# Two more feature pairs of the up projection by seven products of half-width blocks

## The chip, the cores and the metric

One core of a Trainium2 chip runs the whole program. TensorE (PE in the rows, PEld for its weight loads) multiplies, VectorE (DVE) and ScalarE (ACT) do the elementwise work and read PSUM, GpSimd (POOL) does small arithmetic and issues some transfers, SyncE (SP) issues most of the transfers. The metric is the device time of one execution in microseconds, as the median of several.

## The reference

Two layers on 512 tokens of width 1024. The part that matters here is the second half of a layer:

```
def conv_ffn(h, w_up, conv_w, conv_b, w_down):
    u = h @ w_up                        # (512, 1024) @ (1024, 5632)
    u = depthwise_conv3(u) + conv_b     # over tokens, three taps
    a, g = jnp.split(u, 2, axis=-1)     # 22 blocks of 128 features each
    return (jax.nn.gelu(g) * a) @ w_down
...
for l in range(2):
    x = x + gated_parallel_mixer(rmsnorm(x), ...)
    x = x + conv_ffn(rmsnorm(x), ...)
return rmsnorm(x)
```

Everything is float32. Each operand of a product is split into a high part in the fast matmul format (fp32r) and a low part, the rest; a product is the sum of high by high, low by high and high by low, three matmuls for each block of 128 along the contraction.

## The kernel before

The 1024 features of `h` lie as 8 tiles of 128 partitions by 512 tokens, each as a pair (high, low). The FFN width is cut into 22 blocks of 128 features; block f of the plain half ("a") has the number f, that of the gate half ("g") the number 22 + f. `schedule` writes the whole layer as one list of steps by hand, and a parallel list of weight blocks ("specs") in the order in which TensorE uses them. TensorE and SyncE keep that written order (`manual_schedule`). In the stretch of the change VectorE and ScalarE don't: a scheduler orders their instructions when the program is built, by priorities that the code gives (`high_priority`), and that order is then fixed; each engine takes its instructions one after another.

**A normal step** (`("up", f)`, `do_up`) takes one weight block of 1024 by 128: 8 blocks of the contraction by 3 matmuls of 128x512, into one PSUM bank. Then `conv` runs on the block: ScalarE writes the middle tap and the bias into `c` (L1113), VectorE adds the two outer taps (L1115, L1116), ScalarE takes the gelu of a gate block (L1120), VectorE multiplies it with the plain block (`prod`, L215), and after every second block `operands` makes from `prod` the split operands (`ft`) for the down projection (L1141 to L1155).

**A step by seven products** (`("us", i, p)`, `do_us`) computes two neighbouring blocks, 2i and 2i+1, at once. The contraction is cut in its even and its odd blocks (four each), the output in two feature blocks, and the tokens in two halves of 256, so that the result is a 2 by 2 product of blocks, done as 7 products instead of 8. Each product is 4 blocks by 3 matmuls of 128x256. It uses four PSUM banks; the pieces are gathered by ScalarE (L1071 to L1081) and VectorE (L1075, L1079, L1084) in two tiles `u`, of which there are two, and `conv` then reads `u`. The three matmuls of a block are these:

```
mm(ps, wh, hi, ...)    # L1066: high weights, high operand
mm(ps, wh, lo, ...)    # L1067
mm(ps, wl, hi, ...)    # L1068: the low part of the weights
```

The weights of the seven products are, in order, V11, S1, V12, S2, S4, V22 and S3. The V are blocks of the matrix, the S are sums of them. `load_sum` fetches V22 and V11 into tiles `own` (4 of them), V21 into a tile `s` and a tile `raw`, V12 into a `raw` (3 of them); POOL issues two transfers that add in place (V22 onto `s`, which gives S1, L173; V11 onto the second V21, which gives S3, L174); VectorE makes S2 from S1 and V11 (L189) and S4 from S2 and V12 (L192). So in rows `own`, `s` and `raw` as the source of a `wlo` tell which product it is for: own, s, raw, s, raw, own, raw.

**The weight split.** Every spec, normal or of a product, goes through `split`: ScalarE writes the high part `whi` (L208), VectorE the low part `wlo` (L209). There are three tiles of each, so a split can run at most three specs ahead of TensorE: the part for a spec is written when the matmuls of the third spec before it are done. A normal block is 128x1024, a block of a product 128x512.

**The operands of `us`**: `whole` copies the h tiles together into `hx` (8 ScalarE copies, L1025, and 8 transfers by POOL that add the low part in place, L1026), and `mix` makes from each of the four pairs of tiles the sums that the seven products need (`hs`, from `sums4`, L1044 to L1049). They are made once in a layer, beside the blocks 13 and 14, and serve every `us` of the layer.

Order of the second part of the up projection in a layer: after four steps of the down projection (`("sum", 0, m)`) come 13a, 13g, 14a, 14g, ..., 17a, 17g, then 18a, 19a, the one `us` for 18g and 19g, then 20a, 20g, 21a, 21g, and then `cover` and `rest` of the down projection.

**Banks.** `banks` sets for each stage which of the 8 PSUM banks a group of results goes through in turn. `do_mla_open` sets it at the start of a layer: `g` for the first four results (`ps_g`), `d` for the following, `r` for the sums of the norm.

**The constant**: `self.eps` is one column of the tile `cst`; its first reader is ScalarE in `norm_direct` (L495), in the FFN.

Of the kernel before, what the change touches and what calls it, by code (L numbers as in the profile page):

```python
# [24 lines left out]
EPS = 1e-6  # L25
# [14 lines left out]
NP, AHEAD, EVAC = (6, 5, 4), (7, 4), 400  # L40
F2 = 2 * NP[0]
FIX = 6
UPS = ((9, 1),)
ORDERS = (("V11", "S1", "V12", "S2", "S4", "V22", "S3"), ("V11", "V12", "S1", "S2", "S4", "V22", "S3"))
B11, B21, B22, T1, T3, T2, T4 = range(7)
ROWS = (slice(0, 64), slice(64, 128))
# [19 lines left out]
class Trunk:  # L66
# [5 lines left out]
    def __init__(self, ctx, tc, d):  # L72
        self.tc, self.nc, self.d, self.ctx = tc, tc.nc, d, ctx
        nc = self.nc
        self.small = ctx.enter_context(tc.tile_pool(name="small", bufs=1))
        self.const = ctx.enter_context(tc.tile_pool(name="const", bufs=1))
        self.wp = ctx.enter_context(tc.tile_pool(name="wp", bufs=1))
        self.psum = ctx.enter_context(tc.tile_pool(name="psum", bufs=1, space=bass.MemoryType.PSUM))
        self.groups, self.turn = {}, {}
        c = self.const  # L80
        x0 = c.tile([P, S + NPC], F32, name="x0")
        self.x = [x0[:, :S]] + [c.tile([P, S], F32, name=f"x{k}") for k in range(1, KD)]
        self.par = [x0[:, S:], self.small.tile([P, NPC], F32, name="par1")]
        self.early = c.tile([P, P], F32, tag="acc", name="early")
        nc.vector.memset(self.early, 1.0)
        self.idf = c.tile([P, P], F32, name="idf")
        make_identity(nc, self.idf)
        self.mean = c.tile([P, P], F32R, name="mean")
        cst = self.small.tile([P, 7], F32, name="cst")
        self.neghalf, self.ones = cst[:, 0:4], cst[:, 4:5]  # L90
        nc.vector.memset(self.neghalf, -0.5)
        nc.vector.memset(self.ones, 1.0)
        self.eps = cst[:, 6:7]
        nc.vector.memset(self.eps, EPS)
        self.warm = cst[:, 5:6]
        nc.scalar.activation(self.warm, self.ones, AF.Exp)
        self.specs, self.raws, self.parts, self.used = [], {}, [], 0
        self.plans = [self.schedule(l) for l in range(L)]
        for s, W in self.plans:
            self.specs += [w for item in s for w in W.get(item, ())]  # L100
        nc.sync.dma_start(x0[:, :S + PC_CW], d["x0"])
        self.fetch(1, 0)
        for k in range(1, 5):
            nc.sync.dma_start(self.x[k], d["xT"][k * P:(k + 1) * P, :])
            self.fetch(min(k + 1, 3), 0)
        self.gmask = self.small.tile([P, 3 * P], BF16, name="gmask")
# [223 lines left out]
    def schedule(self, l):  # L330
# [30 lines left out]
        for f in ups[8:]:  # L361
            W["up", f] = [(d["w_up"][l], 0, KD, f * P, P)]
        for i, p in UPS:
            unit = {"w": d["w_up"][l], "m": p * NF + 2 * i, "part": 1, "np": 4, "r0": 0, "order": ORDERS[0]}
# [33 lines left out]
        seq[n - 8:n - 8] = [("sum", 0, m) for m in range(0, KD, 2)]  # L398
        for i, p in UPS:
            old = [("up", p * NF + 2 * i + e) for e in range(2)]  # L400
# [97 lines left out]


    def do_mla_open(self):  # L500
        self.banks(g=[0, 1, 2, 3], d=[4, 5, 0, 1, 2, 3], r=[6, 7])
        self.mxs, self.mx = self.open("mx")
        self.mps, self.mp = self.open("ml")
        self.mp2 = self.mps.enter_context(self.tc.tile_pool(name=f"mm{self.l}", bufs=1, reuse_waits="tile"))
        self.rc, self.rsn = (self.mp.tile([P, S], F32, tag=t, name="rope", bufs=2) for t in ("knh", "knl"))
        if self.l:
            self.rope_table()
        self.hb = self.small.tile([P, 24], F32, tag="hb", name="hb")
        self.nc.vector.tensor_scalar(self.hb, self.pr[:, PC_BG:PC_BG + 24], 0.5, None, ALU.mult)
        self.merged, self.z = [None] * KD, {}  # L510
        self.qn, self.kn, self.pts, self.pp, self.y = {}, {}, {}, {}, {}
# [27 lines left out]
    def do_lat4(self):  # L539
        if self.l == 0:  # L540
            rest = self.par[0][:, PC_CW:]
            for t, src in ((rest, self.d["par"][0][:, PC_CW:]), (self.par[1], self.d["par"][1])):
                self.nc.gpsimd.tensor_copy(t[:, 0:4], self.rt)
                self.nc.gpsimd.dma_start(t, src)
            self.nc.gpsimd.tensor_scalar(self.mean, self.idf, 0.0, 1.0 / D, ALU.mult, ALU.add)
        self.latent(4, self.dense(self.spec(), self.h))

# [609 lines left out]
    def do_sum(self, part, m):  # L1157
# [33 lines left out]
        elif m == KD - 2:  # L1191
# [3 lines left out]
            for _ in self.operands(F2):  # L1195
                pass
            if UPS:
                self.whole()
# [219 lines left out]
```

## Time and profile before

| | |
|---|---|
| median of 3 runs | 1665.04 us (1664.78 to 1665.18) |
| the profiled execution: its time | 1664.89 us |
| its span, first to last instruction | 1663.1 us |
| PE busy | 1654.7 us, 99% of the span, 9480 matmuls |
| DVE busy | 1291.4 us, 78%, 2256 instructions |
| ACT busy | 948.3 us, 57%, 1704 instructions |
| POOL busy | 134.1 us, 8% |
| DMA | 191.22 MB, mean 115 GB/s |

A row of the timeline gives the start, the duration, the engine, the line, the operation and "out<-in" by the program's names with the shape; in square brackets stands how long the engine was idle before it and what ended that. Rows of equal instructions that follow each other are merged (x8). A duration of VectorE or ScalarE overlaps a little with the next instruction's, so that what an instruction takes of its queue is read from the distance of the starts. A row by windows gives, for a stretch of time, the busy time of each engine with the number of its instructions, the granted TensorE clock, the busy share of the DMA engines and GB/s.

### The profile page before, as it was taken

To read this page: it belongs to the slowest core of one execution; us is meant where nothing else is said; L and a number is where in the kernel's file an instruction comes from. 1 tells how busy PE (TensorE), PEld (TensorE's weight loads), DVE (VectorE), ACT (ScalarE), POOL (GpSimd) and SP (SyncE) were. 2 spreads that over 40 slices of the span, in tenths; PEclk is the share of its full clock that TensorE was granted. 3 is DMA by queue.
4 is the path that set the end of the run, shared out by engine and by line. 5 is a ranking of instruction groups with operands and counts; after the bars stand their busy time and mean duration, and the time that the engine had idled before them with its cause. 6 is when DMAs were issued, how large, how long until landed. Compare 5 with 4: busy or idle time off the path is not lost.

```text
span 1663.1 us, 25448 instructions
## 1 busy us (share of the span) xinstructions
PE 1654.7 (99%) x9480; PEld 1415.9 (85%) x9480; DVE 1291.4 (78%) x2256; ACT 948.3 (57%) x1704; POOL 134.1 (8%) x190
## 2 busy tenths in 40 slices
PE   9999999999999999999999999999999999999998
PEld 8888888888898889888987888888889888898888
DVE  7767866787889877797967677667878897777887
ACT  7664545775565544555566545467755655436554
POOL 2122100000000000100011220000001000001000
PEclk9999999999999999999999999999999999999999
DMA  6255523222534366636432564332236343657373
GB/s 183 74 125 114 139 84 95 77 77 74 140 97 133 101 149 155 153 96 165 110 105 80 112 146 106 98 89 77 64 85 150 90 127 101 164 131 175 96 168 94
DMA packets 326923, 191.22 MB, mean 115 GB/s; under 512 B 17072, under 2 KB 313792, under 8 KB 326800
## 3 DMA queue, kind: packets, MB, share of 16 engines
q1 hardware_dynamic: 304064, 162.38, 34.8%
q0 software_dynamic: 22448, 26.89, 9.6%
q8 instruction: 74, 1.21, 0.3%
q14 instruction: 49, 0.40, 0.1%
q10 hardware_dynamic: 288, 0.33, 0.1%
HBM read 168.80 MB, written 2.10 MB: 103 GB/s over the span
## 4 chain that ended last, share of the span: by engine, by line
PE 97%; DVE 1%; ACT 1%; issue 0%; DVEq 0%; ACTq 0%
PE ps_ring L222 13%; PE ps_ring L223 12%; PE ps_ring L224 12%; PE ps_d L222 9%; PE ps_d L224 9%; PE ps_d L223 9%; PE ps_d L1177 5%; PE ps_d L1176 5%; PE ps_d L1175 5%; PE ps_g L222 2%; PE ps_g L224 2%; PE ps_g L223 2%; PE ps_ring L303 2%; PE ps_ring L290 1%; PE ps_ring L792 1%; PE ps_g L323 1%
## 5 line engine op out<-in xcount | busy, mean ns | idle before, releaser
L208 ACT CAST whi<-raw 128x1024 fp32r<-128x1024 f32 (+5 forms) x353 | 291.3, 826 | 351.2 <-PE ps_ring L223 123.4
L209 DVE TENSOR_TENSOR wlo<-raw,whi 128x1024 fp32r<-128x1024 f32 (+5 forms) x351 | 331.4, 946 | 79.4 <-ACT whi L208 77.2
L222 PE MATMUL ps_ring<-hh,whi 128*128 128x512 f32 x600 | 235.6, 393 | 0.6 <-DVE pt L761 0.3
L224 PE MATMUL ps_ring<-hh,wlo 128*128 128x512 f32 x600 | 234.0, 390 | 0.0
L223 PE MATMUL ps_ring<-hl,whi 128*128 128x512 f32 x600 | 233.7, 390 | 0.0
L222 PE MATMUL ps_d<-hh,whi 128*128 128x512 f32 x589 | 229.4, 389 | 0.0
L223 PE MATMUL ps_d<-hl,whi 128*128 128x512 f32 x589 | 229.4, 389 | 0.0
L224 PE MATMUL ps_d<-hh,wlo 128*128 128x512 f32 x589 | 229.3, 389 | 0.0
L1176 PE MATMUL ps_d<-ft,whi 128*128 128x256 f32 x546 | 154.7, 283 | 0.0
L1177 PE MATMUL ps_d<-ft,wlo 128*128 128x256 f32 x546 | 154.7, 283 | 0.0
L1175 PE MATMUL ps_d<-ft,whi 128*128 128x256 f32 x546 | 154.7, 283 | 0.0
L222 PEld LDWEIGHTS ps_ring<-hh,whi 128*128 128x128 f32 x600 | 112.7, 188 | 24.8 <-DVE pt L761 0.6
L224 PEld LDWEIGHTS ps_ring<-hh,wlo 128*128 128x128 f32 x600 | 112.7, 188 | 23.7
L223 PEld LDWEIGHTS ps_ring<-hl,whi 128*128 128x128 f32 x600 | 112.7, 188 | 23.0
L224 PEld LDWEIGHTS ps_d<-hh,wlo 128*128 128x128 f32 x589 | 110.6, 188 | 23.1
L222 PEld LDWEIGHTS ps_d<-hh,whi 128*128 128x128 f32 x589 | 110.6, 188 | 22.7
L223 PEld LDWEIGHTS ps_d<-hl,whi 128*128 128x128 f32 x589 | 110.6, 188 | 22.7
L1176 PEld LDWEIGHTS ps_d<-ft,whi 128*128 128x128 f32 x546 | 104.9, 192 | 0.2
L1175 PEld LDWEIGHTS ps_d<-ft,whi 128*128 128x128 f32 x546 | 104.9, 192 | 0.2
L1177 PEld LDWEIGHTS ps_d<-ft,wlo 128*128 128x128 f32 x546 | 104.9, 192 | 0.0
L215 DVE TENSOR_TENSOR gz<-ps_ring,rb 128x512 f32<-128x512 f32 x44 | 30.4, 691 | 63.2 <-PE ps_ring L224 63.2
L222 PE MATMUL ps_g<-hh,whi 128*128 128x512 f32 x176 | 68.9, 391 | 0.9 <-DVE x L1185 0.9
(419 smaller groups left out, 3578.8 us busy)
## 6 DMA issues: line engine op xcount, KB each, us to landing
raw<-in_w_in_dram SPq DMA_DIRECT2D x86, 512.0 KB, 4.0
raw<-in_w_up_dram SPq DMA_DIRECT2D x68, 512.0 KB, 3.8
raw<-in_w_up_dram SPq DMA_DIRECT2D x36, 256.0 KB, 2.9
raw<-in_w_down_dram SPq DMA_DIRECT2D x18, 384.0 KB, 4.9
tm<-in_namask_dram SPq DMA_DIRECT2D x16, 384.0 KB, 4.3
tm<-in_rpb_dram POOLq DMA_DIRECT2D x48, 128.0 KB, 4.7
own<-in_w_down_dram SPq DMA_DIRECT2D x16, 384.0 KB, 5.9
raw<-in_w_in_dram SPq DMA_DIRECT2D x17, 256.0 KB, 3.2
```

The lines of the kernel that those rows point to most:

```text
L208: nc.scalar.copy(hi, src)
L209: nc.vector.tensor_sub(lo, src, r32(hi))
L215: self.nc.vector.tensor_tensor(out, a, b, ALU.mult)
L222: mm(ps, sh, mh, start=first and k == 0, stop=False)
L223: mm(ps, sh, ml, start=False, stop=False)
L224: mm(ps, sl, mh, start=False, stop=last and k == n - 1)
L290: self.nc.tensor.transpose(out[2 * u + i][:, c * 64:c * 64 + 64], block[q], self.idf[q, q])
L303: self.nc.tensor.matmul(out, st[a], mv[b], start=first and t == 0, stop=last and t == 2)
L323: self.nc.tensor.matmul(self.gbank[j], w[:, j * P:(j + 1) * P], m, start=n + t == 0, stop=False)
L1175: mm(ps, wh, hi, start=fresh and i == 0, stop=False, skip_group_check=True)
L1176: mm(ps, wh, lo, start=False, stop=False, skip_group_check=True)
L1177: mm(ps, wl, hi, start=False, stop=i == n - 1, skip_group_check=True)
```

## The change

In each of the two layers the pairs 16g, 17g and 18a, 19a are computed by seven products too, beside 18g, 19g. The steps then stand as ..., 15a, 15g, 16a, 17a, `us` for 16g and 17g, `us` for 18a and 19a, `us` for 18g and 19g, 20a, 20g, 21a, 21g: three such steps in a row (below: the first, the second and the third group). The write of `eps` moves from VectorE at the very start to POOL in `do_lat4` of the first layer. In the second layer `do_mla_open` takes the banks in the order in which the last stage used them, oldest first, instead of fixed numbers.

```diff
-UPS = ((9, 1),)
+UPS = ((8, 1), (9, 0), (9, 1))
...
         self.eps = cst[:, 6:7]
-        nc.vector.memset(self.eps, EPS)
...
     def do_mla_open(self):
-        self.banks(g=[0, 1, 2, 3], d=[4, 5, 0, 1, 2, 3], r=[6, 7])
+        a = [0, 1, 2, 3, 7, 4, 5, 6]
+        if self.l:
+            a = [self.groups["d"][(self.turn["d"] + i) % 8] for i in range(8)]
+        self.banks(g=a[:4], d=[*a[5:7], *a[:4]], r=[a[7], a[4]])
...
     def do_lat4(self):
         if self.l == 0:
...
                 self.nc.gpsimd.dma_start(t, src)
+            self.nc.gpsimd.memset(self.eps, EPS)
             self.nc.gpsimd.tensor_scalar(self.mean, self.idf, 0.0, 1.0 / D, ALU.mult, ALU.add)
```

`schedule` reads `UPS`, and replaces the two normal steps of a pair by one `us` at the place of the second:

```
for i, p in UPS:
    old = [("up", p * NF + 2 * i + e) for e in range(2)]
    seq[seq.index(old[1])] = ("us", i, p)
    seq.remove(old[0])
```

What this makes of the queues is shown at three places of the first layer; the second layer reads alike. Line numbers of the changed kernel are lower by 1 from L95 to L500, higher by 2 from there to L543 and by 3 behind that (its L208 is L209 before, its L1050, L1051, L1118 and L1119 are L1047, L1048, L1115 and L1116 before).

VectorE, where the first group's weights begin. Before, from the sums of the third `mix` on (`wlo` is the low part of a normal block, 17a and then 17g):

```order
L1047 SCALAR_TENSOR_TENSOR tt<-tt,hx 128x256
L209 TENSOR_TENSOR wlo<-raw,whi 128x1024
L1048 SCALAR_TENSOR_TENSOR tt<-tt,hx 128x256
L1044 TENSOR_TENSOR tt<-hx 128x512
L1115 SCALAR_TENSOR_TENSOR c<-ps_d,x_67,c 128x511
L209 TENSOR_TENSOR hs<-tt,hs 128x512
L1116 SCALAR_TENSOR_TENSOR c<-ps_d,x_67,c 128x511
L209 TENSOR_TENSOR hs<-tt,hs 128x512
L1047 SCALAR_TENSOR_TENSOR tt<-tt,hx 128x256
L1048 SCALAR_TENSOR_TENSOR tt<-tt,hx 128x256
L209 TENSOR_TENSOR wlo<-raw,whi 128x1024
```

Now, at the same place (`own` is V11 and `s` is S1 of the first group):

```order
L1050 SCALAR_TENSOR_TENSOR tt<-tt,hx 128x256
L208 TENSOR_TENSOR wlo<-own,whi 128x512
L1051 SCALAR_TENSOR_TENSOR tt<-tt,hx 128x256
L1047 TENSOR_TENSOR tt<-hx 128x512
L1118 SCALAR_TENSOR_TENSOR c<-ps_d,x_67,c 128x511
L208 TENSOR_TENSOR hs<-tt,hs 128x512
L1119 SCALAR_TENSOR_TENSOR c<-ps_d,x_67,c 128x511
L208 TENSOR_TENSOR hs<-tt,hs 128x512
L1050 SCALAR_TENSOR_TENSOR tt<-tt,hx 128x256
L214 TENSOR_TENSOR prod<-c 128x512
L1051 SCALAR_TENSOR_TENSOR tt<-tt,hx 128x256
L208 TENSOR_TENSOR wlo<-s_7379,whi 128x512
```

Up to the first of these rows the queue of VectorE is the same in both kernels; from it on the blocks of 1024 give way to blocks of 512, and the multiplication into `prod` moves ahead of the next split.

VectorE around the last group of the layer (before, the only one), from the low part of its third product (V12) on. Before:

```order
L209 TENSOR_TENSOR wlo<-raw,whi 128x512
L1115 SCALAR_TENSOR_TENSOR c<-ps_d,x_67,c 128x511
L192 TENSOR_TENSOR raw<-s_7539,raw 128x512
L209 TENSOR_TENSOR wlo<-s_7539,whi 128x512
L1116 SCALAR_TENSOR_TENSOR c<-ps_d,x_67,c 128x511
L209 TENSOR_TENSOR wlo<-raw,whi 128x512
L1075 TENSOR_TENSOR u<-u,ps_d 128x256
```

Now, for the third group (L188 and L191 make S2 and S4, L1078 and L1087 gather results, L1158 is the end of `operands` for 16 and 17):

```order
L208 TENSOR_TENSOR wlo<-raw,whi 128x512
L1119 SCALAR_TENSOR_TENSOR c<-u,x_67,c 128x511
L1158 TENSOR_TENSOR ft<-tt,ft 128x512
L188 TENSOR_TENSOR s_7694<-s_7694,own 128x512
L1118 SCALAR_TENSOR_TENSOR c<-u,x_67,c 128x511
L1078 TENSOR_TENSOR u<-u,ps_d 128x256
L191 TENSOR_TENSOR raw<-s_7694,raw 128x512
L1119 SCALAR_TENSOR_TENSOR c<-u,x_67,c 128x511
L208 TENSOR_TENSOR wlo<-s_7694,whi 128x512
L208 TENSOR_TENSOR wlo<-raw,whi 128x512
```

Between the low part of the third product (V12) and that of the fourth (S2) there were two instructions, L1115 and L192; now there are seven, the work of the second group and of the pair 16, 17 among them.

SyncE, the transfers of the up projection after the four steps of the down projection. Before:

```order
L140 DMA raw<-in_w_up_dram 128x8x128 x12
L170 DMA own<-in_w_up_dram 128x4x128
L170 DMA s_7539<-in_w_up_dram 128x4x128
L170 DMA own<-in_w_up_dram 128x4x128
L170 DMA raw<-in_w_up_dram 128x4x128 x2
L140 DMA raw<-in_w_up_dram 128x8x128 x4
```

Now, the third group's shown up to its last `own`:

```order
L139 DMA raw<-in_w_up_dram 128x8x128 x8
L169 DMA own<-in_w_up_dram 128x4x128
L169 DMA s_7379<-in_w_up_dram 128x4x128
L169 DMA own<-in_w_up_dram 128x4x128
L169 DMA raw<-in_w_up_dram 128x4x128 x2
L169 DMA own<-in_w_up_dram 128x4x128
L169 DMA s_7527<-in_w_up_dram 128x4x128
L169 DMA own<-in_w_up_dram 128x4x128
L169 DMA raw<-in_w_up_dram 128x4x128 x2
L169 DMA own<-in_w_up_dram 128x4x128
L169 DMA s_7694<-in_w_up_dram 128x4x128
L169 DMA own<-in_w_up_dram 128x4x128
```

Four blocks of 512 KB give way to ten of 256 KB in a layer, two of them into `raw` for each group; POOL's queue gets four more transfers that add in place, behind the eight of L1026.

## The prediction

> **What bounds the kernel now.** I read the page first, for the bound and the chain that ended last; then the busy times by windows around the place of the change; then the timelines of TensorE and VectorE there.
>
> ```profile
> span 1663.1 us, 25448 instructions
> PE 1654.7 (99%) x9480; PEld 1415.9 (85%) x9480; DVE 1291.4 (78%) x2256; ACT 948.3 (57%) x1704; POOL 134.1 (8%) x190
> PE 97%; DVE 1%; ACT 1%; issue 0%; DVEq 0%; ACTq 0%
> ```
>
> TensorE is the bound nearly everywhere, 97% of the chain. So fewer matmul columns shorten the program only as long as no other queue makes TensorE wait, and a wait put into TensorE's queue is lost for good. Whether VectorE has room must be read where the change lies. The windows of the first layer are four normal steps each, then the group of seven products (745.28 to 755.35), then four normal steps (us, then busy time and number of instructions of each engine, clock, DMA share, GB/s):
>
> ```profile
> core 0: us, PE busy (x) PEld busy (x) DVE busy (x) ACT busy (x) POOL busy (x), PEclk, DMA share, GB/s
> 679.97:701.74 21.77, 21.77 (x98) 18.04 (x97) 12.88 (x19) 13.53 (x22) 7.07 (x8) 1.00 0.96 210
> 701.74:723.51 21.77, 21.77 (x97) 18.03 (x96) 21.74 (x36) 13.28 (x19) 0.49 (x1) 1.00 0.48 135
> 723.51:745.28 21.77, 21.77 (x98) 18.03 (x96) 19.09 (x30) 10.67 (x17) 1.23 (x2) 1.00 0.30 71
> 745.28:755.35 10.07, 10.07 (x85) 10.07 (x84) 7.83 (x12) 7.38 (x13) 0.00 (x0) 1.00 0.34 99
> 755.35:777.12 21.77, 21.77 (x98) 18.04 (x97) 19.00 (x27) 11.80 (x18) 0.86 (x1) 1.00 0.55 155
> ```
>
> This is the reading that decides: TensorE never stops, but VectorE works 21.74 of 21.77 us from 701.74 on. Its 78% over the span hide a stretch in which it is full. Why it is full stands in its timeline (first row: 7.80 us idle, ended by the landing of the additions into `hx`; by then it is late with all that needs them). The same row of the second layer:
>
> ```profile
> 690.75 0.69 DVE L1044 TENSOR_TENSOR tt<-hx 128x512 f32<-128x512 f32 x1 [7.80 <-DMA hx<-hl]
> ...
> 1514.48 0.69 DVE L1044 TENSOR_TENSOR tt<-hx 128x512 f32<-128x512 f32 x1 [7.59 <-DMA hx<-hl]
> ```
>
> Less 823.93 us, the distance of the two stages (1503.90 and 679.97), the second is 690.55, so both layers start this stretch alike to 0.2 us. Before the change VectorE catches up in the normal steps up to 745 and the group finds it with room. After it the first group stands where 16g would end, at 723.51: in the full stretch.
>
> **The change part by part.**
>
> *TensorE's own time.* The rows at the start of the second up stage, at the start of the group and behind it:
>
> ```profile
> 679.97 0.40 PE L222 MATMUL ps_d<-hh,whi 128*128 128x512 f32 x1
> ...
> 745.28 0.28 PE L1066 MATMUL ps_d<-hh,whi 128*128 128x256 f32 x1
> ...
> 755.35 0.40 PE L222 MATMUL ps_d<-hh,whi 128*128 128x512 f32 x1
> ```
>
> Between the first two lie 12 normal steps of 24 matmuls: 65.31 us, 5.442 us a step, 0.2268 us a matmul. The group's 84 matmuls take 10.07 us, 0.1199 each, 1.439 us a product. A pair costs 10.88 us in normal steps and 10.07 us as a group: 0.81 us saved, four pairs in two layers, **-3.25 us**. The page "TensorE: Matmul & The Clock Gate" of the Trainium skill (section Back-to-back issue gap) gives N / 2.4 + 2.5 ns for a gap, 109 and 216 ns here; by that a pair would save 48 x 0.216 - 84 x 0.109 = 1.2 us, four 4.8 us. The trace has some 11 ns more for every matmul of either width, and the sum goes by the trace.
>
> *VectorE's queue.* What an instruction takes of it is the distance of the starts:
>
> ```profile
> 715.15 0.42 DVE L1047 SCALAR_TENSOR_TENSOR tt<-tt,hx 128x256 f32<-128x256 f32 x1
> 715.49 1.22 DVE L209 TENSOR_TENSOR wlo<-raw,whi 128x1024 fp32r<-128x1024 f32 x1
> 716.62 0.43 DVE L1048 SCALAR_TENSOR_TENSOR tt<-tt,hx 128x256 f32<-128x256 f32 x1
> 716.96 0.69 DVE L1044 TENSOR_TENSOR tt<-hx 128x512 f32<-128x512 f32 x1
> 717.56 0.75 DVE L1115 SCALAR_TENSOR_TENSOR c<-ps_d,x,c 128x511 f32<-128x511 f32 x1
> 718.22 0.69 DVE L209 TENSOR_TENSOR hs<-tt,hs 128x512 fp32r<-128x512 f32 x1
> ```
>
> 0.34 us for 256 columns, 0.60 for 512, 0.66 for a tap of the convolution, 1.13 for 1024. Two normal steps give it two splits of 1024 and four taps, 2 x 1.13 + 4 x 0.66 = 4.9 us in 10.88 us. A group gives it seven splits (4.2), S2 and S4 (1.2), two gathers of 256 and one of 512 (1.28), and four taps (2.64): 9.3 us in 10.07 us, and beside that the products and operands of 16 to 19 (two `prod`, L1141, and two of 256 and four of 512 for a pair, 4.9 us). So the change trades 0.81 us of TensorE for 4.4 us of VectorE, four times, and packs it into 30 us.
>
> Now the due times. The queue up to L1047 at 715.15 is the same in both kernels, and the first new instruction, the low part of V11 of the first group, starts at 715.49 too. From there to the low part of the fourth product (S2) of the third group, 67 instructions stand in the built order: 20 low parts of 512 (17 products and three `hs`), six S sums, three `prod`, eight of `operands`, two gathers L1084, the last L1044 and the first L1141, together 41 of 512; 14 taps of seven blocks; 12 of 256. That is 41 x 0.60 + 14 x 0.66 + 12 x 0.34 = 37.9 us, and the 68th starts at 753.4 at the earliest and is done 0.69 us later. TensorE, never waiting, would be at that product after 17 products from 723.51, 747.97, and use its low part with its third matmul, at 748.2. Adding 0.1 us for the signal (below, 829.42 to 829.56) it is there at 754.2: **6.0 us late** if VectorE never idles.
>
> It idles a little, for reasons that these rows of the group before show (a gelu late, a split's high part late, a gather that waits for its product):
>
> ```profile
> 738.00 0.69 DVE L215 TENSOR_TENSOR prod<-c 128x512 f32<-128x512 f32 x1 [0.76 <-ACT c L1120]
> ...
> 751.76 0.69 DVE L209 TENSOR_TENSOR wlo<-raw,whi 128x512 fp32r<-128x512 f32 x1 [0.70 <-ACT whi L208]
> 752.74 0.42 DVE L1079 TENSOR_TENSOR u<-u,ps_d 128x256 f32<-128x256 f32 x1 [0.28 <-PE ps_d L1068]
> ```
>
> In the new order L1079 of the first group stands behind the splits of its sixth and seventh product, so VectorE waits there for the fifth product; `prod` of 17 stands right behind the taps and waits for its gelu; one split behind L1079 waits for ScalarE. With one such wait of each kind in the 67 instructions, 0.3 + 0.7 + 0.3 (half of the third, since ScalarE has most of the gather's time for it), I take 1.3 us; the ends are 0 and 3 us (all three kinds in two of the groups, 2 x 1.74 less what overlaps). So TensorE loses **7.3 us a layer, 14.6 us** (12.0 to 18). Along the way it waits in smaller pieces, first at the third product of the first group, whose low part is the 20th of the 68 and due at 726.6 where VectorE is done with it at about 726.8; the largest, about 3 us, is the last, at S2 of the third group, behind the seven instructions that now stand there. Behind it come four normal steps, in which VectorE has 5.44 us for 3.7 us of work (1.13 + 2 x 0.66 + 4.9 / 4), and nothing more is lost.
>
> *Transfers.* Ten blocks of 256 KB for four of 512 KB in a layer, in SP's written order, and four more additions on POOL:
>
> ```profile
> raw<-in_w_up_dram SPq DMA_DIRECT2D x36, 256.0 KB, 2.9
> own<-in_w_up_dram SPq DMA_DIRECT2D x4, 256.0 KB, 4.6
> s<-own POOLq DMA_DIRECT2D x2, 256.0 KB, 3.3
> ```
>
> The DMA share is 0.30 to 0.48 where they fall, so bandwidth covers them. The tightest is V12 of the second group: its `raw` is free when S3 of the first is split (about 732), it lands 3 to 4 us later and is due on VectorE at about 737. I take nothing; if it is late it moves VectorE by up to 1 us a group, which is part of the upper end. POOL's additions come behind the eight into `hx` and 3.3 us land well ahead of use: nothing.
>
> *Other banks.* At the start of the second layer TensorE's last matmul of the first, the VectorE instruction that empties its bank, and the first of the second:
>
> ```profile
> 828.41 0.28 PE L1177 MATMUL ps_d<-ft,wlo 128*128 128x256 f32 x1
> 828.73 0.69 DVE L1185 TENSOR_TENSOR x<-x,ps_d 128x512 f32<-128x512 f32 x1
> 829.56 0.47 PE L222 MATMUL ps_g<-hh,whi 128*128 128x512 f32 x1 [0.87 <-DVE x L1185]
> ```
>
> The distance is 1.15 us where 0.12 is the rule. The first four results of the layer go to banks 0 to 3, which the last step still held. Oldest first, they find empty banks: **-1.03 us**. Two more groups also move the turn by four banks, so even the fixed numbers would miss them now. The ends are 0 and -1.03.
>
> *The constant.* A row of 0.06 us leaves VectorE, which then waits for `x` anyway; on POOL it stands behind the first write of `idf`, where POOL idles 8 us:
>
> ```profile
> 0.97 0.06 DVE L94 MEMSET cst<- 128x1 f32 x1
> ...
> 3.73 0.35 DVE L468 TENSOR_SCALAR h<-x 128x256 fp32r<-128x256 f32 x1 [2.49 <-DMA x<-in_x_dram]
> ...
> 9.00 0.76 POOL masks.py:199 TENSOR_SCALAR_AFFINE_SELECT idf<-idf 128x128 f32<-128x128 f32 x1 [8.06 <-issue]
> ...
> 21.90 0.60 PE L251 MATMUL ps_r<-idf,acc 128*128 128x128 f32 x4
> ```
>
> Nothing; `idf` has 12 us of cover, without which it could cost 0.1 us.
>
> *The sum*: -3.25 - 1.03 + 14.6 = +10.3 us on the profiled execution's 1664.89, which is 0.15 below the median of the runs: 1675.2, and against the median 1675.3. Bounds: 12.0 - 4.28 gives 1672.6, 18 - 3.25 gives 1679.6.
>
> **The rivals.**
>
> *VectorE is early enough, and the columns count.* All hangs on one time, the landing of `hx`. If the eight additions landed 7.3 us earlier than 690.75, VectorE would use that idle row and be in time at the third group; the kernel would gain 4.28 us, 1660.8, about 0.26% (0.2%, some 3 us, is what a measurement of this kernel can tell from no change). For it: the transfers in that window (DMA share 0.96) would only have to be fewer. Against it: up to 695 the same transfers stand in the same order on both queues, and the groups' own come later. At some 5 us earlier the stalls that are left, 2.1 us a layer, balance the gain: 1664 to 1666.
>
> *The clock falls.* The first rows of TensorE in the trace:
>
> ```profile
> 1.05 3.36 PE L432 MATMUL idle<-early 128*128 128x128 f32 x14 [1.05 <-DVE cst L92]
> ...
> 4.44 2.04 PE L323 MATMUL ps_g<-h,whi 128*128 128x512 f32 x4
> ```
>
> After the idle start TensorE is slow: four matmuls of 512 in 2.04 us, one each 0.5 us against 0.227 later, though it has worked since 1.05, so for some 5 us. If a wait in the groups brings that state back, 5 us of products at half speed lose 2.5 us a layer, 1680.3. The longest wait that I expect, 3 us, is longer than any of the trace before, so whether it is long enough isn't shown; the granted clock of 1.00 in the windows speaks against it only for shorter ones. The same page of the Trainium skill (section HAM oscillation) has a rule for it: no idle gaps of more than about 3.4 us, or the clock halves. By that rule a wait of 3 us is just short enough.
>
> *The banks do nothing.* If the first results of the second layer wait for a weight split instead, the 1.03 us stay, 1676.3. Against it: the high part of its first block is written 3 us before (first row), only that of the third falls into the wait:
>
> ```profile
> 825.01 0.62 ACT L208 CAST whi<-raw 128x512 fp32r<-128x512 f32 x1 [1.07 <-PE ps_d L1176]
> ...
> 828.65 0.62 ACT L208 CAST whi<-raw 128x512 fp32r<-128x512 f32 x1 [1.18 <-PE ps_d L1176]
> ```
>
> **How the numbers follow.** The forecast, 0.77; VectorE early enough 0.05, or half so 0.05; the clock 0.06; the banks 0.07. Faster by over 0.2% is the first rival alone, 0.05; within 0.2% the half of it, 0.05; slower 0.90. The range takes in the bounds of the forecast, the clock and the banks, and stretches below the bound of 1672.6 for a VectorE that goes 3% faster through its queue (1.1 us a layer): 1670.4 to 1680.
>
> **What the profile after would show.** VectorE without a gap of a microsecond from 690 to about 757 in the first layer and again some 829 us later (823.93, and what the first layer loses); in the list of waits TensorE waiting for `wlo` L208 in the three groups, 7 us a layer, most of it at the fourth product of the third group; the groups at 0.12 us a matmul between the waits; no wait for L1188 (L1185 before) at the start of the second layer. I am wrong if TensorE passes the third group without waits, or if the 67 instructions take clearly other than 38 us.

## The result, and the profile after

The changed kernel takes **1678.86 us** (median of 4 runs, 1677.86 to 1679.58) where the kernel before takes 1665.10 on the same chip: a ratio of 1.0083, 95% interval 1.0065 to 1.0100. It is 13.8 us slower; the forecast was 1675.3, 10.3 us slower, and the measured time lies inside its range. The profiled execution is the one of 1679.58 us, 14.7 us above the profiled one of before.

The head of its page, the bound and the chain:

```profile
span 1677.8 us, 25906 instructions
PE 1657.4 (99%) x9624; PEld 1422.6 (85%) x9624; DVE 1307.6 (78%) x2295; ACT 962.5 (57%) x1740; POOL 141.5 (8%) x199
PE 89%; DVE 7%; issue 2%; ACT 1%; DMA 1%; POOL 0%; DVEq 0%; ACTq 0%
```

TensorE's share of the span hides the loss again, but the chain doesn't: VectorE had 1% of it before, and has 7% now. Where, the windows of the first layer say (the stretches of before; the three groups now stand from 723.46 to 762.84):

```profile
701.74:723.51 21.77, 21.77 (x98) 18.03 (x97) 21.77 (x39) 12.88 (x22) 3.45 (x4) 1.00 0.69 141
723.51:745.28 21.77, 18.22 (x145) 17.46 (x144) 20.70 (x36) 14.03 (x27) 1.72 (x2) 1.00 0.41 99
745.28:755.35 10.07, 7.93 (x64) 7.52 (x62) 10.07 (x19) 6.68 (x13) 0.00 (x0) 1.00 0.16 47
755.35:777.12 21.77, 21.38 (x109) 18.94 (x110) 17.77 (x26) 13.23 (x20) 0.00 (x0) 0.92 0.44 128
```

VectorE is full, TensorE has holes, 3.55 us in the second row and 2.14 in the third. The last row shows what none of the windows of before above had: a granted clock of 0.92. The list of waits of TensorE (in total, how often, the longest), and after it TensorE's own rows in the first layer:

```profile
PE ps_d L1071 <- DVE wlo L208: 5.9, 5, 2.0
PE ps_d L1069 <- ACT u L1076: 4.8, 2, 2.4
PE ps_d L1069 <- ACT whi L207: 0.8, 1, 0.8
```

```profile
726.90 0.39 PE L1071 MATMUL ps_d<-hh,wlo 128*128 128x256 f32 x1 [0.17 <-DVE wlo L208]
731.29 0.39 PE L1071 MATMUL ps_d<-hh,wlo 128*128 128x256 f32 x1 [0.99 <-DVE wlo L208]
743.77 0.38 PE L1069 MATMUL ps_d<-hh,whi 128*128 128x256 f32 x1 [2.39 <-ACT u L1076]
753.53 0.39 PE L1069 MATMUL ps_d<-hs,whi 128*128 128x256 f32 x1 [0.82 <-ACT whi L207]
755.74 0.46 PE L1071 MATMUL ps_d<-hs,wlo 128*128 128x256 f32 x1 [1.71 <-DVE wlo L208]
```

These are the third and the fifth product of the first group, the fifth of the second, and the fourth of the third (twice). The wait for L1188 at the start of the second layer is gone.

To set these apart from a slow clock I take the distance of the starts of neighbouring matmuls in the groups. A distance above 0.12 us is a wait; the excess of matmuls that run at half clock is counted by itself. That gives 7.7 us of waits in the first layer and 6.7 in the second, and 1.46 and 1.49 us for the clock. The account of the 14.7 us: columns -3.25, banks -1.03, waits +14.4, clock in the groups +2.95, the very end +1.2, 0.4 in small pieces. The very end is the stretch behind TensorE's last matmul. The windows of the last work, before and after, have the same busy time of TensorE:

```profile
1609.23:1663.10 53.87, 48.71 (x408) 48.26 (x406) 41.38 (x77) 28.86 (x48) 1.73 (x2) 0.99 0.34 98
1622.70:1677.80 55.10, 48.72 (x408) 48.27 (x406) 41.41 (x77) 28.90 (x48) 1.73 (x2) 0.97 0.34 97
```

From the end of the last matmul to the end of the span it takes 5.01 us before and 6.18 after; there the last transfers of the output land, and the lower clock of the second row falls there too, where no matmul is left to slow. This stretch has 5.0 to 7.5 us in the profiled executions of this case, and 5.26 in e_groups below, which has the same groups. So these 1.2 us are scatter and no effect of the groups.

### The profile page after: what moved, and what is told of

The parts are those of the page before. It is cut to its first block, busy times and chain, and to the rows that moved or that the text cites. A ratio compares the mean times of both kernels' runs of the same rounds, so it can differ in the third digit from the quotient of the medians.

```text
span 1677.8 us, 25906 instructions
## 1 busy us (share of the span) xinstructions
PE 1657.4 (99%) x9624; PEld 1422.6 (85%) x9624; DVE 1307.6 (78%) x2295; ACT 962.5 (57%) x1740; POOL 141.5 (8%) x199
## 4 chain that ended last, share of the span: by engine, by line
PE 89%; DVE 7%; issue 2%; ACT 1%; DMA 1%; POOL 0%; DVEq 0%; ACTq 0%
PE ps_ring L221 13%; PE ps_ring L222 12%; PE ps_ring L223 12%; PE ps_d L223 7%; PE ps_d L221 7%; PE ps_d L222 7%; PE ps_d L1179 5%; PE ps_d L1178 5%; PE ps_d L1180 5%; PE ps_g L223 2%; PE ps_g L221 2%; PE ps_g L222 2%; PE ps_ring L302 2%; DVE wlo L208 2%; PE ps_ring L289 1%
## 5 line engine op out<-in xcount | busy, mean ns | idle before, releaser
L208 DVE TENSOR_TENSOR wlo<-raw,whi 128x1024 fp32r<-128x1024 f32 (+5 forms) x355 | 329.7, 931 | 77.7 <-ACT whi L207 75.7
L223 PE MATMUL ps_d<-hh,wlo 128*128 128x512 f32 x525 | 204.3, 389 | 0.0
L222 PE MATMUL ps_d<-hl,whi 128*128 128x512 f32 x525 | 204.3, 389 | 0.0
L221 PE MATMUL ps_d<-hh,whi 128*128 128x512 f32 x525 | 204.3, 389 | 0.0
L223 PEld LDWEIGHTS ps_d<-hh,wlo 128*128 128x128 f32 x525 | 98.6, 188 | 20.7 <-DVE wlo L208 0.2
L222 PEld LDWEIGHTS ps_d<-hl,whi 128*128 128x128 f32 x525 | 98.6, 188 | 20.5
L221 PEld LDWEIGHTS ps_d<-hh,whi 128*128 128x128 f32 x525 | 98.6, 188 | 20.2
L223 PE MATMUL ps_g<-hh,wlo 128*128 128x512 f32 x176 | 68.8, 391 | 0.0
```

What stands on the lines that cost most here:

```text
L208: nc.vector.tensor_sub(lo, src, r32(hi))
L221: mm(ps, sh, mh, start=first and k == 0, stop=False)
L222: mm(ps, sh, ml, start=False, stop=False)
L223: mm(ps, sl, mh, start=False, stop=last and k == n - 1)
```

## The experiments

Medians are given with the ratio to runs of the kernel before on the same chip (its medians there: 1665.34 to 1665.77). "Waits" are counted as above, for the first and the second layer. Where an edit touches VectorE's work, its order is built anew and differs in some places too.

| kernel | median us | ratio, 95% interval | waits | clock in the groups |
|---|---|---|---|---|
| changed | 1678.86 | 1.0083 (1.0065 to 1.0100) | 7.7, 6.7 | 1.5, 1.5 |
| e_banks | 1665.54 | 1.0001 (0.9992 to 1.0010) | 0, 0 | none |
| e_groups | 1680.61 | 1.0092 (1.0078 to 1.0106) | 7.1, 6.3 | 1.5, 3.0 |
| e_fill | 1676.22 | 1.0067 (1.0051 to 1.0082) | 7.7, 7.5 with the filler | none |
| e_u2own | 1675.56 | 1.0065 (1.0051 to 1.0078) | 6.4, 6.0 | none |
| e_nohxadd | 1678.18 | 1.0079 (1.0065 to 1.0093) | 5.5, 6.0 | 2.9, 1.5 |
| e_nohx_u2 | 1672.23 | 1.0039 (1.0024 to 1.0054) | 4.2, 4.3 | 1.2, 0 |
| e_notaps | 1667.11 | 1.0012 (1.0003 to 1.0021) | 2.4, 2.6 | none |
| e_8_9 | 1673.90 | 1.0050 (1.0036 to 1.0064) | 4.6, 5.4 | 0, 1.5 |
| e_90_91 | 1669.80 | 1.0025 (1.0016 to 1.0034) | 2.7, 2.7 | 1.5, 1.5 |
| e_9_10 | 1668.49 | 1.0021 (1.0012 to 1.0030) | 0.7, 0.9 | none |
| e_pool | 1686.01 | 1.0120 (1.0103 to 1.0136) | 8.7, 8.5 | 3.5, 3.4 |
| e_pool_u2 | 1683.68 | 1.0110 (1.0095 to 1.0125) | 8.5, 8.4 | 2.4, 2.4 |

**The banks and the constant alone** (e_banks, from the changed kernel):

```diff
-UPS = ((8, 1), (9, 0), (9, 1))
+UPS = ((9, 1),)
```

> Only the bank order and the place of the small constant are new; the group of seven products is the one for 18g, 19g as before. Theory (the term of the prediction): 1.03 us less than before, 1664.0 us, because TensorE's wait for the instruction that empties its bank at the start of the second layer goes; the distance there falls from 1.15 us to about 0.12. Rival (another wait, for a weight split, takes its place): 1665.0, with a distance of about 1.1 us and another releaser.

The time doesn't move (1.0001). TensorE's rows at the start of the second layer and 56 us later say why:

```profile
830.89 0.28 PE L1180 MATMUL ps_d<-ft,wlo 128*128 128x256 f32 x1
831.01 0.40 PE L221 MATMUL ps_g<-hh,whi 128*128 128x512 f32 x1
...
887.94 0.47 PE L221 MATMUL ps_ring<-mg,whi 128*128 128x512 f32 x1 [0.69 <-DVE ev L214]
```

The wait at the start is gone, distance 0.12. But 56 us later a new result (`ps_ring`) waits for `ev`, an instruction of VectorE that reads an older result out of PSUM and that itself waits for a broadcast by POOL. `ev` starts as late behind the layer's start as before (56.1 us; before, 56.4), where no matmul waited for it, and 0.79 of the 1.03 us is lost there. From the group of the first layer to that of the second it takes 823.86 us, before 823.93, so 0.07 of the gain is left. Both theories were half right: the term was there, and most of it was given back elsewhere. In the changed kernel, whose turn of the banks is another, the same place shows no wait.

**The groups alone** (e_groups, from the kernel before):

```diff
-UPS = ((9, 1),)
+UPS = ((8, 1), (9, 0), (9, 1))
```

> Only the two more groups of seven products, with the fixed bank numbers and the constant as before. Theory: two more groups move the turn of the banks by eight places in all, so the fixed numbers now find banks that are empty, and the time is that of the whole change, 1677.9 to 1679.6 us, with 0.12 us at the start of the second layer. Rival (the oldest-first order is what takes the wait away there): 1.03 us longer than the whole change, near 1679.9, with the wait of about 1 us still in the trace.

```profile
836.59 0.28 PE L1177 MATMUL ps_d<-ft,wlo 128*128 128x256 f32 x1
836.71 0.40 PE L222 MATMUL ps_g<-hh,whi 128*128 128x512 f32 x1
```

Fixed bank numbers, and yet a distance of 0.12: the two groups shift the turn, and that alone takes the wait away. The median is 1.0 us above the theory's range; its profiled execution has three windows at half clock in the groups, one more than the changed kernel's. Within both intervals the time is that of the whole change, so no gain of the bank order with these groups can be told.

**Work in the gaps** (e_fill):

```diff
+            if (f2, p, j) in ((9, 0, 4), (9, 1, 3)):
+                for _ in range(20):
+                    mm(banks[3], self.h[0][0][:, 0:P], self.h[0][0][:, first], start=True, stop=True, ...)
```

> The changed kernel, with 20 added matmuls of 256 columns (some 2.4 us, their result is overwritten and not used) on TensorE ahead of the fifth product of the second group and ahead of the fourth product of the third, where the changed kernel waits 2.55 and 2.85 us. Theory (the waits bring the clock down): the stretches of 3.41 us at half clock at 755.9 and 1575.1 us go, the two layers lose some 1.5 us each less, and the time is about 1675.7 us; what TensorE loses to waits and filler together stays near 7 us a layer. Rival A (the clock falls for another reason, the load or the tail): the two stretches stay, 1678.9. Rival B (the filler itself is in the way): no half clock, but 2 to 4 us longer in the groups, 1678 to 1680.

The theory holds: 80 matmuls more, and 2.6 us less than the changed kernel's median; the granted clock of the whole execution is 1.000 in its four runs, 0.996 or 0.997 in those of the changed kernel. Of the 3.15 us between the profiled executions 2.2 lie in the groups and 0.9 behind the last matmul. Its windows over the two former gaps and behind them:

```profile
742.20:745.61 3.41, 3.41 (x29) 3.21 (x28) 2.95 (x6) 1.53 (x4) 0.00 (x0) 1.00 0.40 107
752.44:755.85 3.41, 3.02 (x26) 2.82 (x25) 3.41 (x7) 1.97 (x4) 0.00 (x0) 1.00 0.00 0
755.85:759.26 3.41, 3.41 (x29) 3.41 (x30) 2.14 (x4) 1.68 (x4) 0.00 (x0) 1.00 0.49 143
```

TensorE is kept busy and the clock stays at 1.00; waits and filler together still come to 7.7 and 7.5 us. So the waits brought the clock down, and the lateness behind them is not TensorE's.

**A third tile u** (e_u2own):

```diff
+        if (f2, p) == (9, 0):
+            u2 = self.const.tile([P, S], F32, tag="sq0", name="u")
```

> The changed kernel, but the second tile u of the second group is a third one (a tile that is free there), so that the copy which empties the second bank doesn't wait for the convolution of the first group. Theory (VectorE's queue is the bound, and the wait at the fifth product of the second group is only the place where part of its lateness shows): that wait of 2.55 us falls below 0.5, the waits for the weights of the third group grow by about as much, the sum stays at 6 to 8 us a layer, and the time within 2 us of the changed kernel, the clock's part included. Rival (the tile u is a bound of its own): 2.5 us less in each layer and no half clock in the second, 1671 to 1674.

In the changed kernel the fifth product of the second group needs a PSUM bank that ScalarE empties with L1076 (into the second tile `u`); this copy waits for the first group's convolution, whose last tap stands late in VectorE's queue. VectorE's and ScalarE's rows of the changed kernel:

```profile
742.50 0.75 DVE L1119 SCALAR_TENSOR_TENSOR c<-u,x,c 128x511 f32<-128x511 f32 x1
...
743.34 0.38 ACT L1076 ACTIVATE u<-ps_d 128x256 f32<-128x256 f32 x1 [1.14 <-DVE c L1119]
```

With the third tile the wait of 2.55 us falls to 0.57, now for a `wlo`, and the third group takes over a part: e_u2own's list has one entry in place of three,

```profile
PE ps_d L1073 <- DVE wlo L208: 8.6, 11, 1.6
```

and the sum of the waits falls by about 1.4 and 0.7 us where 2.0 went at the one place. So neither side has it whole: the time, 1675.56, is 3.3 us below the changed kernel's, more than the theory's 2 and short of the rival's range. The order built anew has a part in it: 64 instructions stand in VectorE's queue from the first group's V11 to the third's S2, and take 37.2 us, where the changed kernel has 67 and 39.4. No single wait is over 1.8 us, and the clock stays up. That the time is nearly the forecast's is partly luck: the waits come to 12.4 us and not to 14.6, and the stretch behind the last matmul is 2.4 us longer than before in its profiled execution.

**VectorE 8 us earlier** (e_nohxadd; the sums for the products leave out the low parts):

```diff
-            self.nc.gpsimd.dma_start(part, r32(self.h[k][1]), accum_op=ALU.add)
```

> The changed kernel without the eight transfers of a layer that add the low parts in place to hx (the sums for the seven products are made of the high parts alone). Theory (everything hangs on the landing of hx): VectorE's idle row of 7.8 us at 690 goes, so it stands some 7 us earlier in its queue at the first group, the waits of about 7 us a layer fall below 1 us, no stretch at half clock in the groups, and the time is 1661 to 1663. Rival A (the lateness comes from the groups themselves, 28 us of VectorE's work in 30 us, whenever they begin): waits of 3 us or more a layer stay, 1667 or more. Rival B (the tile u is a bound of its own): the wait of 2.5 us at the fifth product of the second group stays whole, 1666 to 1668.

The theory falls, and rival A is nearest. VectorE's rows of this run, and one of ScalarE:

```profile
682.88 0.68 DVE L1046 TENSOR_TENSOR tt<-hx 128x512 f32<-128x512 f32 x1
...
686.34 1.29 DVE L208 TENSOR_TENSOR hs<-tt,hs 128x512 fp32r<-128x512 f32 x2 [1.86 <-ACT hs L207]
...
691.97 1.23 DVE L208 TENSOR_TENSOR wlo<-raw,whi 128x1024 fp32r<-128x1024 f32 x1 [1.49 <-ACT whi L207]
...
712.60 0.62 ACT L207 CAST whi<-own 128x512 fp32r<-128x512 f32 x1 [1.71 <-PE ps_d L222]
713.87 0.69 DVE L208 TENSOR_TENSOR wlo<-own,whi 128x512 fp32r<-128x512 f32 x1
...
754.27 0.68 DVE L208 TENSOR_TENSOR wlo<-s,whi 128x512 fp32r<-128x512 f32 x1
```

It starts on `hx` 7.95 us earlier than in the changed kernel (690.83), but the lead doesn't keep: VectorE soon waits for ScalarE's high parts. The high part of V11 itself can't come earlier: ScalarE's row at 712.60 waits for TensorE, which only then is done with 15g, the third spec before, and gives back its tile of the three. So the tiles of the split cap the lead; in both layers of this run V11's low part starts 9.6 us ahead of the group, in the changed kernel 7.9 and 8.3. At the first group it is 1.7 us earlier (713.87 against 715.58), at S2 of the third 0.74 us (754.27 against 755.01). The waits of the first group go (1.6 to 2 us a layer), those of the second and third stay, and the clock falls three times in the groups.

**Both** (e_nohx_u2: the two edits above together):

> The changed kernel without the transfers that add the low parts to hx (the sums are made of the high parts alone) and with a third tile u for the second group. Theory A (the late start of VectorE costs only the first group's 2 us, the tile u about 1 us, and the rest is work that doesn't fit): 3.5 to 5 us of waits a layer, no single one over 1.9 us, no half clock, 1668 to 1671. Theory B (late start and tile are the whole cause): waits below 1 us a layer, 1661 to 1663.

4.2 and 4.3 us of waits stay: theory A, though the time is 1.2 us above its range. The profiled execution, at 1672.97, has one window at half clock (1.2 us) and 1.0 us more than before behind the last matmul; what put the median above the range isn't shown. Late start and tile are not the whole cause.

**Less work for VectorE** (e_notaps; the two outer taps of the convolution are left out for the blocks of the groups):

```diff
-        for _ in self.conv(fi, u):
+        for _ in self.conv(fi, u, False):    # False: without L1118 and L1119
```

> The changed kernel without the two outer taps of the convolution for the blocks of the three groups: twelve VectorE instructions of 0.66 us fewer in a layer, eight of them (5.3 us) ahead of the fourth product of the third group. Theory (TensorE waits for the sum of VectorE's work): the waits of the first group, about 1.7 us, stay, since all eight come behind them; of the rest, some 5.3 us, nothing is left; no half clock in the groups; 1664 to 1666. Rival (the waits hang on single dependences, a tile or a sum, and not on the amount of work): waits of 5 us or more a layer stay, 1673 or more.

5.3 us of instructions fewer, and 5.3 us of waits fewer in the first layer (7.7 to 2.4), 4.1 in the second; what stays is the first group's wait of 1.14 us and small ones, no half clock. The median, 1667.1, lies 1.1 us above the theory's range, and far below the rival's. The run takes away more than work: the copy L1076 no longer has a tap to wait for, so amount and this one dependence are not apart in it. But e_nohx_u2 has that dependence removed too and keeps 4.2 us a layer, with all the taps. Together they show that TensorE waits for the amount of VectorE's work.

**The same work on POOL** (e_pool, and e_pool_u2 with the third tile u):

```diff
+        add = (self.nc.gpsimd if unit["part"] == 1 and w == 512 else self.nc.vector).tensor_add
-            self.nc.vector.tensor_add(unit["S2"], unit["S1"], unit["V11"])
+            add(unit["S2"], unit["S1"], unit["V11"])
...
-        self.mul(self.prod[:, i:i + S], self.ca.pop(f), c)
+        (self.nc.gpsimd if 16 <= f < 20 else self.nc.vector).tensor_tensor(self.prod[:, i:i + S], self.ca.pop(f), c, ALU.mult)
```

> The changed kernel with the sums S2 and S4 of the three groups and the four products prod of 16 to 19 on POOL instead of VectorE: ten instructions of 0.60 us fewer in VectorE's queue in a layer, eight of them (4.8 us) ahead of the fourth product of the third group; the output is the same. Theory (TensorE waits for the sum of VectorE's work, microsecond for microsecond, as without the taps): 2 to 2.8 us of waits a layer stay, no half clock in the groups, 1665 to 1667.5. Rival (POOL is too slow: a row of 128 columns takes it 0.6 us, so 512 may take over 2 us, and S2 and then S4 stand ahead of the weight splits): the waits only change their name, 5 us or more a layer, 1672 or more.

> The same, and the second group's second tile u is a third one. Theory (the tile u adds something of its own only where VectorE is late): within 1 us of the run without it, 1664.5 to 1667.5. Rival (the tile is what is left of the waits behind the first group): 1 to 1.5 us less in each layer, 1663 to 1664.5, which would be the first version with the groups that beats the kernel before.

The theory falls, and the rival's signs come: waits of 8.7 and 8.5 us, and a time well over 1672. The tile makes 2.3 us of difference by the clock, not by the waits. The timeline of e_pool, both engines, in the second group:

```profile
740.06 0.62 ACT L208 CAST whi<-s 128x512 fp32r<-128x512 f32 x1 [2.60 <-POOL s L189]
740.28 1.88 POOL L1130 TENSOR_TENSOR prod<-c 128x512 f32<-128x512 f32 x1
740.71 3.23 DVE L209 TENSOR_TENSOR wlo<-s,whi 128x512 fp32r<-128x512 f32 x1 [3.35 <-ACT whi L208]
741.52 1.86 POOL L192 TENSOR_TENSOR raw<-s,raw 128x512 f32<-128x512 f32 x1
```

A split that takes VectorE 0.69 us takes 3.23 here, as long as POOL works on `prod` and the sum: the engine that was to be relieved is held up, which I had not expected. (The split of the third group, beside one sum of POOL, takes 1.78.) And ScalarE and VectorE wait first for POOL's S2 (2.60 and 3.35 us idle). TensorE then waits 2.9 us for that split, and the clock is halved for 10.24 us. The page "SBUF — State Buffer" of the Trainium skill (section Who interferes with whom) has the rule that a VectorE instruction with two SBUF inputs and a GpSimd instruction that reads SBUF shut each other out of a shared port, the second one until the first is done. These rows agree that the split waits; it waits for two instructions of POOL, the second of which starts after it.

**Two groups instead of three.** 16g, 17g and 18g, 19g (e_8_9), 18a, 19a and 18g, 19g (e_90_91), 18g, 19g and 20g, 21g (e_9_10):

```diff
-UPS = ((8, 1), (9, 0), (9, 1))
+UPS = ((8, 1), (9, 1))     # or ((9, 0), (9, 1)), or ((9, 1), (10, 1))
```

> Two groups instead of three: 16g, 17g and 18g, 19g by seven products, with the two normal steps 18a, 19a between them; banks and constant as in the change. Theory (VectorE starts the first group without any lead, and two normal steps behind it give it 10.9 us for 9.8 us of work): the waits of the first group stay as in the whole change, 1.7 to 2 us a layer, the last group has none; two pairs save 1.6 us and the banks up to 1.0, so 1666 to 1667, and no half clock. Rival (each added group costs the same, half of what the whole change loses): 3.5 us of waits a layer, 1669 to 1671.

> Two groups, 18a, 19a and 18g, 19g by seven products, one right behind the other and none for 16g, 17g; banks and constant as in the change. Theory (two separate causes: the late start at 723.5 us costs a group that stands there 2 us, and two groups in a row hold some 24 us of VectorE's work in 20 us, of which its spare time from 723 to 734 us covers one or two): no wait in the first of the two, 2 to 3 us a layer in the second, no half clock; two pairs save 1.6 us and the banks 0.2 to 1.0, so 1667 to 1669.5. Rival (every added group costs the same wherever it stands, as 16g, 17g alone did with 4.6 and 5.2 us of waits): 1673 to 1674.5.

> The second group stands where VectorE has room: 18g, 19g and 20g, 21g by seven products, with the normal steps 20a, 21a between them; banks and constant as in the change. Theory (the place decides: from 755 to 777 us VectorE works 19.0 of 21.8 us, so the 4.4 us more make it at most 1.5 us late, which its lead over TensorE covers): waits below 1 us a layer; two pairs save 1.6 us and the banks 0.2 to 1.0, 1662.5 to 1664. Rival (any second group in a layer makes VectorE late): 2 us or more of waits a layer, 1667 or more.

e_8_9 misses my number by 7 us and its rival's by 3: not only the first group waits (1.9 and 1.7 us), the last one does too (2.7 and 3.6 us), with the 10.9 us of the normal steps between them used up by what the first group leaves behind. One more group, in the full stretch, costs 60% and 80% of the waits of two more. e_90_91 shows the place: without the late start the first of two groups has no wait and the second 2.7 us, as expected; the clock, which I had not expected, took another 1.5 us a layer in the profiled execution (1670.67), and the median, 1669.8, is just outside my range. Its 11 runs show what the clock does: the one with a granted clock of 1.000 took 1668.21 us, the five with 0.997 took 1669.99 to 1671.73. In e_9_10 the groups come out as expected (0.7 and 0.9 us), and the time doesn't: it is slower by 0.21%. TensorE's rows in its last down projection:

```profile
1613.07 0.39 PE L1179 MATMUL ps_d<-ft,whi 128*128 128x256 f32 x1 [0.43 <-DVE ft L1152]
1616.55 0.39 PE L1180 MATMUL ps_d<-ft,wlo 128*128 128x256 f32 x1 [0.94 <-DVE wlo L208]
1619.29 0.39 PE L1179 MATMUL ps_d<-ft,whi 128*128 128x256 f32 x1 [1.16 <-DVE ft L1158]
```

By the distances of the starts these three waits cost 3.0 us. The operands `ft` of the last pair are late for the end of the kernel: the lateness moved on to the next stage. I had read VectorE's room up to 777 us and not asked who needs the work after it. None of these versions beats the kernel before.

## Why the prediction was right, and where it was not

**The sign and the mechanism were right.** VectorE's queue sets the pace in the groups. The two rows on which the sum rests, in the changed kernel:

```profile
715.58 0.68 DVE L208 TENSOR_TENSOR wlo<-own,whi 128x512 fp32r<-128x512 f32 x1
...
755.01 0.68 DVE L208 TENSOR_TENSOR wlo<-s,whi 128x512 fp32r<-128x512 f32 x1
```

The 67 instructions took 39.4 us (40.3 in the second layer); the forecast had 37.9 and 1.3 of idle time, 39.2. TensorE went on at 755.74, the forecast gives 755.5. The first wait came at the third product of the first group at 726.90, as written. The waits were to cost 14.6 us and cost 14.4. The same reckoning holds for the runs with another queue: with 58 instructions ahead of S2 that take 34.3 us (e_notaps) that split is 2.4 us late for a TensorE that never waits, with 61 and 37.0 us (e_nohx_u2) 3.5, and the waits of the first layer are 2.4 and 4.2 us.

**Columns, transfers and constant** came out: 0.12 us a matmul between the waits, no wait for a transfer or the constant. **The banks** came out in size (-1.03) at their place; e_groups shows that the groups' own shift of the turn did it, which the prediction named as a second reason, and e_banks that the same edit without the groups gains nothing.

**Where the waits fall was partly wrong.** The largest was to be the last, about 3 us at S2 of the third group. There stand 0.98 and 1.87; a wait of 2.55 us stands at the fifth product of the second group, by the tile `u`, which I had not followed: VectorE's lateness also holds tiles and banks. e_u2own shows that it is in part a place and not a cause: of 2.0 us a layer that went there, 0.6 and 1.3 came back elsewhere.

**"All hangs on one time, the landing of hx" was wrong.** The first rival rested on it: additions 7.3 us earlier were to gain the whole loss. e_nohxadd had them 8 us earlier and kept 5.5 and 6.0 us of waits. The step that failed is the assumption that VectorE carries a lead forward: the three tiles of the split cap it, and of 8 us 1.7 were left at the first group. What more tiles would do, no run shows.

**The clock was the term that was mis-sized.** It stood as a rival with 0.06 and 2.5 us a layer, since the longest wait was to be about 3 us and nothing showed whether that is enough. It was: 1.46 and 1.49 us, since the clock stayed down for 3.41 us and not for 5, and e_fill shows the cause. With the 1.2 us behind the last matmul, which are scatter, this is what separates 1675.3 from the profiled 1679.58 us. That the measured time still lies within the forecast's bounds is partly luck: their upper end, 1679.6, was for 18 us of waits, and the clock and the very end took up what the waits left.

## What to carry to other kernels

An engine's mean load says nothing about a place where it is full; reckon its queue from the last instruction that both versions share to the one that the bound engine waits for, and then ask which stage needs the work that is pushed behind. Taking work away from the full engine shortens the waits about one for one (5.3 us for 5.3 in the first layer), while an earlier start of 8 us or another buffer gave back only 0.7 to 2.2 us a layer here, and giving work to POOL made VectorE slower. Where TensorE waits for two microseconds in one place, count the clock as a cost of its own, or keep TensorE busy through the gap.

## What the runs showed of the hardware

**The clock is judged in fixed windows of 3.413 us.** Stretches at half clock in the groups last 3.413 us (or three times that, in e_pool) and begin on a grid: 755.90 and 1575.10 in the changed kernel lie 819.20 us apart, 240 windows; 741.88, 755.54 and 1584.97 in e_nohxadd lie 4 and 243 windows apart. Windows on that grid, of the changed kernel first (granted clock third from the end, TensorE's busy time the second number):

```profile
752.49:755.90 3.41, 0.88 (x5) 0.47 (x5) 3.41 (x7) 2.01 (x4) 0.00 (x0) 1.00 0.00 0
755.90:759.31 3.41, 3.41 (x17) 3.41 (x18) 1.68 (x3) 0.92 (x3) 0.00 (x0) 0.50 0.53 151
1571.69:1575.10 3.41, 1.01 (x8) 0.81 (x8) 2.98 (x6) 1.79 (x4) 0.00 (x0) 1.00 0.58 133
1575.10:1578.51 3.41, 3.41 (x18) 3.41 (x17) 2.95 (x6) 2.48 (x4) 0.00 (x0) 0.50 0.56 157
1585.34:1588.75 3.41, 1.62 (x13) 1.62 (x14) 2.94 (x5) 1.66 (x4) 0.00 (x0) 1.00 0.00 0
```

and of e_8_9:

```profile
1580.06:1583.47 3.41, 1.58 (x13) 1.58 (x14) 3.41 (x7) 1.53 (x4) 0.00 (x0) 1.00 0.00 0
1583.47:1586.88 3.41, 3.41 (x19) 3.41 (x18) 2.43 (x5) 2.02 (x4) 0.00 (x0) 0.50 0.62 174
```

Idle time is counted here as the distance of the starts less 0.12 us. Of the windows at full clock in the groups of these runs, all 16 with 2.0 us of it or more were followed by one at half clock, two of the six between 1.9 and 2.0 were, and none with less. So the next window is slow where TensorE stood still for some 2 of the 3.4 us, and the same wait of 2.5 us costs 1.5 us more or not by how it falls on the grid: the first layer's 2.55 us of the changed kernel fell in two windows (1.02 and 1.53) and cost nothing, the second layer's fell in one. That is one reason why the runs of these kernels scatter by 1 to 5 us. The page "TensorE: Matmul & The Clock Gate" of the Trainium skill has the free-running window of 3413 ns (section What's actually happening), and the trace agrees; its rule of gaps over 3.4 us (section HAM oscillation), which the prediction used, is too wide by this measurement: 2.55 us were enough in one piece, and in e_8_9 1.9 us within a window.

**POOL holds VectorE up** where both have two-input instructions: 0.69 us became 3.23 beside two of POOL and 1.78 beside one (e_pool, above).
